# Hybrid RWKV-7 / short-convolution layer on one core: the stage's cross products come first, operands, blocks and values in half as many transfers

## The chip, the core and the metric

The program runs on one NeuronCore of one Trainium2 chip. TensorE (PE) multiplies matrices, VectorE (DVE), ScalarE (ACT) and GpSimd (POOL) work elementwise, SyncE (SP) issues most of the DMA transfers, which 16 DMA engines carry out. The metric is the device time of one execution in microseconds (us), as the median of several runs. The profile is one further execution, recorded by the hardware profiler; its times count from the first instruction.

## The reference

One denoising step of a one-layer backbone over 128 context tokens and 2048 latent tokens, 1024 channels, in float32. Half of the channels go through a bidirectional RWKV-7 scan (8 heads of 64), the other half through a gated short convolution; both share one input and one output projection.

```python
def step(S, inp):
    r_t, w_t, k_t, v_t, kk_t, a_t = inp
    s_kk = jnp.einsum('bdhij,bdhj->bdhi', S, kk_t)
    S = (S * w_t[..., None, :] - s_kk[..., :, None] * (kk_t * a_t)[..., None, :]
         + v_t[..., :, None] * k_t[..., None, :])
    return S, jnp.einsum('bdhij,bdhj->bdhi', S, r_t)
...
y = ys[:, 0] + jnp.flip(ys[:, 1], axis=1)
...
y = y + (bonus[..., None] * vh).reshape(b, t, A_WIDTH)
...
ya = ya.astype(x.dtype) * jax.nn.silu(g_a)
yb = b_gate * _short_conv(c_gate * u_conv, lp['conv_w'], is_latent) * jax.nn.silu(g_b)
u = jnp.concatenate([ya, yb], axis=-1) @ lp['w_out']
return x + gate * u, s_final
```

The outputs are the normalised context, the normalised latents and the final states of the context scan.

## The kernel before

**Phase 1** projects blocks of 384 tokens through the input weights, forms what the scan needs and writes it to DRAM scratch: `ops0`/`ops1` hold, for each chunk of 64 tokens and direction, the four operands of the chunked scan, `vt` the values, `sg` and `q` the gate and the bonus term, `mixT` the convolution branch. This part is hardly touched by the change.

**Phase 2** is the scan. A *stage* s (17 of them, `NST`) is 128 tokens, two chunks for each of the two directions; one chunk of one direction is a *unit* (s, i, d), four to a stage, in the order of `UNITS`. For a unit:

- `load_unit` (L692) loads `kb` (two operands of all heads, 256 KB) and `x` (two 128 KB loads). `kb` has three buffers, `x` twelve.
- `cross` (L704) multiplies them on PE (tile `psG`, one buffer in PSUM); ACT copies the lower block out (`lab`, L715), four small transfers of 16 KB write its two triangular 32x32 halves to DRAM scratch `at` (L721), DVE masks the rest (`abr`, and back into `x`).
- `turn` (L728) transposes `kb` on PE (`psT`) and ACT copies that out (`kbt`).

After the four units of a stage, `inverse` (L737) loads all its blocks from `at` with 128 partitions (`ab`, L742) and inverts them on POOL by elimination (L747 to L762, one `zt` buffer); POOL itself issues four transfers that write the result to DRAM scratch (L767). `merge` (L817) loads that as `zb` (L821), transposes it on DVE (`ws`, L825) and joins the 32x32 halves to 64x64 blocks with two groups of products on PE (`psU`, `psW`). `step` (L856) then carries the state through one chunk of both directions: products `psw`, `psy`, `pst`, then `psu` with the merged blocks, then the updates of state and output. `load_v` (L847) brings its values, four transfers of 64 KB a chunk.

`main` (L1041) interleaves this: while stage s is stepped, the four units of stage s+2 are crossed and its inversion is started, and at the end of stage s the merge of stage s+1 is done. Between these stand pieces of the output projection (`project`, L1005), six matmuls of 512 columns each: first for the convolution half (`psoc`, 17 tiles, up to stage 8), and from stage 9 on for the scan's half (`psoa`), whose tiles are finished two a stage (`finish`, L953, which loads `sg` and `q`) and then pushed as jobs.

**Order.** On PE the order of phase 2 is the order in which the code is written (`Queue`, L638, ties each PE instruction to the one before). The other engines are ordered by the scheduler when the program is built; on the chip each engine, and SP's queue of transfers, runs strictly in that fixed order. A transfer whose wait is not over holds up all that stand behind it on SP. The built program gives SP's transfers eight completion semaphores in turn, so a transfer also waits for the one eight places before it.

## Time and profile before

| | us |
|---|---|
| median of 3 runs | 1896.28 (1894.37 to 1896.54) |
| the profiled execution | 1894.33 |
| its span, first to last instruction | 1892.4 |
| PE busy | 1636.2 (86%) |
| DVE busy | 1050.6 (56%) |
| ACT busy | 641.0 (34%) |
| POOL busy | 595.5 (31%) |
| DMA queue of SP, share of 16 engines | 63.4% |

The page of the profile also gives the largest groups of transfers: x 136 of 128 KB, kb 68 of 256 KB, the writes of `at` 272 of 16 KB, sv 136 of 64 KB, ab 34 of 256 KB, zb 17 of 512 KB. In a timeline row the columns are start, length, engine, line, operation, output tile <- input tiles, size, count, and in brackets the idle time before it and what ended it; "SPq" is SP's queue issuing a transfer, not the transfer itself. A row of windows gives a stretch of the span, its length, the busy time of each engine (with the count of instructions), the granted PE clock, the busy share of the DMA engines and what they moved. Shares over the whole span mix phase 1, which PE fills, with the scan; the scan is to be read by its stages.

### The profile page before, as it was taken

How to read it: one execution, taken by the hardware profiler on the slowest of the kernel's cores; microseconds unless marked ns; L12 is line 12 of the kernel's file. 1: busy time of each engine (PE TensorE's matmuls, PEld its weight loads, DVE VectorE, ACT ScalarE, POOL GpSimd, SP SyncE). 2: the span in 40 equal slices, each digit the busy share in tenths (PEclk: the TensorE clock that was granted, in tenths of full speed). 3: DMA queues.
4: the chain of work that ended last, by engine and by line, in shares of the span. 5: the costliest groups of instructions: out<-in, count | busy, mean ns of one | idle time of the engine just before them, and what ended most of it. 6: DMA issues, size and time to landing. Idle time of an engine off the chain costs nothing.

```text
span 1892.4 us, 41268 instructions
## 1 busy us (share of the span) xinstructions
PE 1636.2 (86%) x16646; PEld 1427.6 (75%) x16646; DVE 1050.6 (56%) x1883; ACT 641.0 (34%) x1284; POOL 595.5 (31%) x1096
## 2 busy tenths in 40 slices
PE   5999999999999999989898788889577668888777
PEld 2998899998899999888798566667466446666665
DVE  6888877446776354776343535344344335455546
ACT  4555544224443122544110232223123223333323
POOL 0122210002211000222056055564565555555600
PEclk7999999999999999999999888889787778788879
DMA  8789997649889434888864755654555534555433
GB/s 342 226 218 243 225 265 251 210 155 177 189 187 217 147 126 145 192 190 201 256 189 152 209 157 165 179 162 136 177 159 161 158 93 110 163 152 154 133 90 123
DMA packets 395022, 339.93 MB, mean 180 GB/s; under 512 B 289032, under 2 KB 340104, under 8 KB 380752
## 3 DMA queue, kind: packets, MB, share of 16 engines
q1 hardware_dynamic: 392656, 332.84, 63.4%
q0 software_dynamic: 2176, 4.46, 1.3%
q8 instruction: 131, 2.15, 0.5%
q14 instruction: 59, 0.48, 0.1%
HBM read 215.68 MB, written 121.52 MB: 178 GB/s over the span
## 4 chain that ended last, share of the span: by engine, by line
PE 34%; DMA 22%; POOL 19%; DVE 12%; issue 6%; SPq 4%; ACT 2%; POOLq 0%; DVEq 0%; ACTq 0%
POOL zt L762 9%; DMA scr_ops<-sp 6%; POOL ztmp L759 6%; DMA ab<-scr_at 3%; DMA scr_zt<-zt 2%; DMA w<-scr_wsp 2%; PE psoa L648 2%; DMA scr_at<-lab 2%; SPq L721 2%; DMA kb<-scr_ops 2%; PE mmgb L159 1%; PE psoc L648 1%; PE mmgb L161 1%; PE mmgb L160 1%; POOL scr_zt L767 1%
## 5 line engine op out<-in xcount | busy, mean ns | idle before, releaser
L762 POOL TENSOR_TENSOR zt<-zt,ztmp 128x30 f32<-128x30 f32 (+7 forms) x510 | 216.3, 424 | 40.0
L759 POOL TENSOR_TENSOR ztmp<-ab,zt 128x60 f32<-128x60 f32 (+7 forms) x255 | 138.6, 543 | 20.0
L723 DVE TENSOR_TENSOR abr<-psG,mx 128x256 f32<-128x256 f32 x68 | 28.8, 423 | 195.0 <-ACT lab L715 194.8
L315 POOL TENSOR_TENSOR shk<-rawl 128x384 f32<-128x384 f32 (+1 forms) x24 | 26.5, 1106 | 319.9 <-ACT rawl L311 319.9
L648 PE MATMUL psG<-x,kb 64*64 64x128 f32 x2176 | 80.8, 288 | 40.0 <-DMA kb<-scr_ops 30.1
L648 PEld LDWEIGHTS psG<-x,kb 64*64 64x64 f32 x2176 | 63.6, 140 | 54.6 <-issue 48.0
L751 POOL COPY dgp<-ab 128x16 f32<-128x16 f32 x17 | 4.5, 264 | 315.6 <-DMA ab<-scr_at 315.5
L648 PE MATMUL psoa<-woh,mh 128*128 128x512 f32 x136 | 66.1, 486 | 37.7 <-ACT mh L1001 37.7
L726 DVE TENSOR_TENSOR x<-psG,mx 64x512 f32<-64x512 f32 x136 | 93.6, 689 | 1.8
L825 DVE STREAM_TRANSPOSE ws<-zb 32x512 f32<-32x512 f32 x34 | 23.8, 701 | 109.5 <-DMA zb<-scr_zt 101.5
L648 PE MATMUL psU<-ws,lab 32*32 32x32 f32 x1088 | 29.9, 219 | 60.3 <-DVE ws L825 56.2
L648 PEld LDWEIGHTS psU<-ws,lab 32*32 32x32 f32 x1088 | 27.0, 134 | 67.9 <-issue 54.3
L1021 DVE TENSOR_TENSOR o<-psoa,gl 128x512 f32<-128x512 f32 x32 | 21.9, 684 | 88.3 <-PE psoa L648 88.3
L159 PE MATMUL mmk<-h,w 128*128 128x384 f32 (+1 forms) x184 | 62.2, 338 | 8.4 <-DMA w<-scr_wsp 8.4
L159 PE MATMUL mmg<-h,w 128*128 128x384 f32 (+1 forms) x192 | 63.6, 331 | 5.8 <-ACT rawc L318 3.4
L159 PE MATMUL mmv<-h,w 128*128 128x384 f32 (+1 forms) x192 | 66.1, 344 | 1.7 <-ACT q1r L313 1.6
L648 PEld LDWEIGHTS psoa<-woh,mh 128*128 128x128 f32 x136 | 29.1, 214 | 50.8 <-ACT mh L1001 39.9
L159 PE MATMUL mmgb<-h,w 128*128 128x384 f32 (+1 forms) x192 | 64.3, 335 | 1.4 <-DMA w<-scr_wsp 1.4
L735 ACT COPY kbt<-psT 128x512 f32<-128x512 f32 x68 | 39.9, 587 | 73.8 <-PE psT L648 73.5
L159 PE MATMUL mmc<-h,w 128*128 128x384 f32 (+1 forms) x192 | 63.9, 333 | 1.1 <-DMA w<-scr_wsp 1.1
L648 PE MATMUL psoc<-woh,mh 128*128 128x512 f32 x136 | 64.0, 471 | 0.7 <-ACT woh L993 0.7
L648 PE MATMUL psoa<-woh,ml 128*128 128x512 f32 x136 | 61.3, 451 | 3.7 <-DVE ml L1002 3.6
(298 smaller groups left out, 5256.8 us busy)
## 6 DMA issues: line engine op xcount, KB each, us to landing
w<-scr_wsp SPq DMA_DIRECT2D x68, 1024.0 KB, 7.7
scr_wsp<-w SPq DMA_DIRECT2D x34, 1024.0 KB, 6.3
wr<-in_win SPq DMA_DIRECT2D x34, 512.0 KB, 6.9
kb<-scr_ops SPq DMA_DIRECT2D x68, 256.0 KB, 3.9
x<-scr_ops SPq DMA_DIRECT2D x136, 128.0 KB, 4.3
scr_ops<-sp SPq DMA_DIRECT2D x80, 192.0 KB, 4.5
scr_ops<-sp SPq DMA_DIRECT2D x160, 96.0 KB, 5.0
ab<-scr_at SPq DMA_DIRECT2D x34, 256.0 KB, 4.1
```

Source lines behind the costliest of these rows:

```text
L159: T.matmul(ps[:, :n], w[:, 0, k], hh[:, 0, k, :n], start=k == 0, stop=False)
L160: T.matmul(ps[:, :n], w[:, 0, k], hh[:, 1, k, :n], start=False, stop=False)
L315: G.tensor_tensor(s[:, lo:n].rearrange("p (r c) -> p r c", c=64), rp[:, :R, 0:64], rp[:, :R, 2:66], ALU.add)
L648: r = f(*args, **kw)
L721: D(at[u0:u0 + 4, h, b].rearrange("u j i -> j u i"), un.lab[r0:r0 + 32, :, b * 32:b * 32 + 32])
L723: V.tensor_tensor(un.abr[:], pb[:, :, 1, :], B.mx[:, 0, 1].unsqueeze(1).broadcast_to((128, 4, 64)), ALU.mult)
L726: V.tensor_tensor(un.x[q, h].rearrange("r a p t -> r p a t"), px[q], B.mx[q, d].unsqueeze(1).broadcast_to((64, 4, 2, 64)), ALU.mult)
L735: P.copy(un.kbt[:], pt[:])
L759: G.tensor_tensor(tv, ab[:, j:j + 2, j + 2:32].unsqueeze(1).broadcast_to((128, kn, 2, n)), zt[:, :kn, j:j + 2].unsqueeze(3).broadcast_to(( ...
L762: G.tensor_tensor(zt[:, :kn, j + 2:32], zt[:, :kn, j + 2:32], tv[:, :, r], ALU.add)
L825: V.transpose(zr[r0], zb[r0, :, 0:32])
L1021: V.tensor_tensor(o[:], ps[:], g[:, cs], ALU.mult)
```

## The change

Four things, all in phase 2 (plus the layout of `vt`, `at` in scratch).

1. **Fewer, larger transfers.** `load_units` replaces `load_unit` and brings both chunks of a direction at once: `kb` 512 KB in one transfer (two buffers of twice the size), `x` in two of 256 KB (six buffers of twice the size). The blocks `lab` of two units share a tile, and their halves are written to `at` after the second one, 32 KB each. `load_v` brings both directions in one transfer for each half of the heads. Per stage: x 8 to 4, kb 4 to 2, writes of `at` 16 to 8, sv 8 to 4.
2. **Cross products first.** In a stage the crosses and turns of stage s+2 no longer stand between the pieces of projection but right behind the first products of each step.
3. **One slot later.** The third part of a merge (`psW`) moves from the end of stage s into stage s+1, behind the first products of its step; three pieces of projection stand behind the merge instead of one; tiles that are finished wait in a list (`waiting`) and become a job when one of two places is free.
4. **Small ones.** The projection's scratch `o` has one buffer instead of two; the four writes of the inverse (L771) read neighbouring partitions instead of every second one.

```diff
@@ -626,7 +626,7 @@
 for _d in range(2):
     SCR[f"ops{_d}"] = (36, 128, 16, 64)
     SCR[f"pc{_d}"] = (512, 34)
-SCR.update(vt=(17, 2, 128, 4, 64), sg=(512, NT), q=(512, NT), mixT=(512, NT))
+SCR.update(vt=(2, 34, 64, 4, 64), sg=(512, NT), q=(512, NT), mixT=(512, NT))
 
 
...
-    def long(un, shape, tag):
-
-        i = un.n % 12
-        return tl(O.r if i < 8 else O.l, shape, f"{tag}{i}", 1)
-
-    def load_unit(s, i, d):
-        un = Ctx()
-        units[s, i, d] = un
-        un.n = (s * 2 + i) * 2 + d
-        src = S[f"ops{d}"][34 + i if s == 0 and d == 1 else 2 * s + i]
-        un.kb = tl(O.r, [128, 4, 2, 64], "kb", 3)
-        un.x = long(un, [128, 2, 2, 4, 64], "x")
-        D(un.kb[:].rearrange("r p k t -> r (p k) t"), src[:, 8:16])
+    def long(n, of, shape, tag):
+
+        i = n % of
+        return tl(O.r if 3 * i < 2 * of else O.l, shape, f"{tag}{i}", 1)
+
+    def load_units(s, d):
+
+        n = 2 * s + d
+        e = 34 if s == 0 and d == 1 else 2 * s
+        src = S[f"ops{d}"][e:e + 2].rearrange("i r k t -> r i (k t)")
+        kb = tl(O.r, [128, 2, 4, 2, 64], "kb", 2)
+        x = long(n, 6, [128, 2, 2, 2, 4, 64], "x")
+        D(kb[:].rearrange("r i p k t -> r i (p k t)"), src[:, :, 512:1024])
         for h in range(2):
-            D(un.x[HR[h], h].rearrange("r a p t -> r (a p) t"), src[HR[h], 0:8])
-        return un
+            D(x[HR[h], :, h].rearrange("r i a p t -> r i (a p t)"), src[HR[h], :, 0:512])
+        for i in range(2):
+            un = Ctx()
+            units[s, i, d] = un
+            un.n = (s * 2 + i) * 2 + d
+            un.kb, un.x = kb[:, i], x[:, i]
...
-        un.lab = tl(O.r, [128, 4, 64], "lab", 8)
-        P.copy(un.lab[:], pb[:, :, 0, :])
-        at = S["at"][s]
-        u0 = i * 8 + d * 4
+        if i == 0:
+            un.labs = tl(O.r, [128, 2, 4, 64], "lab", 4)
+        else:
+            un.labs = units[s, 0, d].labs
+        un.lab = un.labs[:, i]
+        P.copy(un.lab, pb[:, :, 0, :])
         for h in range(2):
-            for b in range(2):
+            for b in range(2 * i):
                 r0 = h * 64 + b * 32
-                D(at[u0:u0 + 4, h, b].rearrange("u j i -> j u i"), un.lab[r0:r0 + 32, :, b * 32:b * 32 + 32])
-        un.abr = long(un, [128, 4, 64], "abr")
+                x = un.labs[r0:r0 + 32, :, :, b * 32:b * 32 + 32].rearrange("j i p c -> j (i p) c")
+                D(S["at"][s, b, d * 8:d * 8 + 8, h].rearrange("u j i -> j u i"), x)
+        un.abr = long(un.n, 12, [128, 4, 64], "abr")
...
-            D(ab[h * 64:h * 64 + 64].rearrange("p j i -> p (j i)"), at.rearrange("u s b j i -> (u s b) (j i)"))
+            D(ab[h * 64:h * 64 + 64].rearrange("p j i -> p (j i)"), at.rearrange("b u h j i -> (b u h) (j i)"))
...
-                G.dma_start(x, zt[c * 64 + b:c * 64 + 64:2])
+                G.dma_start(x, zt[c * 64 + b * 32:c * 64 + b * 32 + 32])
 
     def first(s):
+        for d in range(2):
+            load_units(s, d)
         for k in UNITS:
-            load_unit(s, *k)
             cross(s, *k)
             yield
             turn(s, *k)
...
-        for d in range(2):
-            c = i if d == 0 else 1 - i
-            for h in range(2):
-                x = S["vt"][tile_of(s, d), h, c * 64:c * 64 + 64]
-                D(sv[HR[1 - h], h, d], x)
+        c = [2 * tile_of(s, 0) + i, 2 * tile_of(s, 1) + 1 - i]
+        e = sorted(c)
+        for h in range(2):
+            x = S["vt"][h, e[0]:e[1] + 1:e[1] - e[0]].rearrange("d t p v -> t d p v")
+            q = sv[HR[1 - h], h]
+            D(q if c == e else q[:, ::-1], x)
...
-            o = tl(O.w, [128, 512], "o", 2)
+            o = tl(O.w, [128, 512], "o", 1)
...
+        def refill():
+            while len(jobs) < 2:
+                if convs:
+                    t = convs.pop(0)
+                    x = tl(O.w, [128, 4, 128], "mr", 1)
+                    D(x[:], S["mixT"][:, t * 128:t * 128 + 128].rearrange("(k p) t -> p k t", p=128))
+                    src, att = A["x"], 0
+                elif B.att and waiting:
+                    t, x = waiting.pop(0)
+                    src, att = S["z0"], 1
+                else:
+                    return
+                z = tl(O.w, [128, 1024], "z", 2)
+                D(z[:], src[t * 128:t * 128 + 128, :])
+                jobs.append(project(t, att, parts(x), z))
+
...
+        def finish_a(k):
+            if k < len(fin):
+                next(fin[k][2])
+
+        def finish_b():
+            if fin:
+                t, y, f = fin.pop(0)
+                next(f)
+                waiting.append((t, y))
+                if B.att:
+                    refill()
 
...
             a = step(s, 0)
             next(a), next(a)
-            Rp(2)
-            L(s + 2, 1)
+            next(m, None)
+            C(0)
+            R(0)
             next(a)
-            piece()
-            Rp(3)
-            L(s + 2, 2)
-            C(0)
-            piece()
-            R(0)
-            L(s + 2, 3)
             C(1)
+            R(1)
             next(a), next(a)
-            piece()
-            finish_piece(True)
+            finish_a(0)
             C(2)
             piece()
-            finish_piece(False)
+            R(2)
+            L(0)
             a = step(s, 1)
             next(a), next(a)
-            piece()
-            next(a)
-            R(1)
+            finish_a(1)
             C(3)
             if u:
                 inverse(u)
+            R(3)
+            L(1)
+            next(a)
             piece()
-            finish_piece(True)
+            finish_b()
+            piece()
             next(a), next(a)
-            finish_piece(False)
             piece()
-            L(s + 3, 0)
-            m = merge(s + 1) if s + 1 < NST else iter(())
-            next(m, None)
-            next(m, None)
+            finish_b()
             piece()
-            next(m, None)
+            if s + 1 < NST:
+                m = merges[s + 1] = merge(s + 1)
+                next(m), next(m)
+            piece(3)
```

**SP's queue in a middle stage**: what stands between the load of one stage's inverse (`zb`) and the load of the next stage's blocks (`ab`). Before:

```order
L821 DMA zb_12592<-scr_zt 128x16x64
L721 DMA scr_at<-lab_12461 32x4x32 x4
L854 DMA sv_12677<-scr_vt 64x256
L943 DMA scr_ysp<-y_12310 128x512
L943 DMA scr_ysp<-y_12312 128x512
L742 DMA ab_12471<-scr_at 64x1024 x2
```

and after the change:

```order
L829 DMA zb_13012<-scr_zt 128x16x64
L728 DMA scr_at<-lab_12617 32x8x32 x4
L699 DMA kb_12766<-scr_ops_57 128x2x512
L701 DMA x_1429_12767<-scr_ops_57 64x2x512 x2
L701 DMA x_1439_12909<-scr_ops_59 64x2x512 x2
L728 DMA scr_at<-lab_12666 32x8x32 x4
L699 DMA kb_12908<-scr_ops_59 128x2x512
L749 DMA ab_12839<-scr_at 64x1024 x2
```

All eight writes of `at` and most of the operand loads of the stage after now stand between the two; before, only the last unit's four writes did.

**SP's queue in a late stage** (around the `zb` of stage 12; `sg` and `mr` are the loads of `finish`). Before:

```order
L721 DMA scr_at<-lab_16758 32x4x32 x4
L699 DMA kb_16790<-scr_ops_59 128x512
L821 DMA zb_17191<-scr_zt 128x16x64
L721 DMA scr_at<-lab_16812 32x4x32 x3
L1036 DMA out_y<-z_16489 128x1024
L721 DMA scr_at<-lab_16812 32x4x32
L854 DMA sv_16926<-scr_vt 64x256 x4
L1074 DMA z_17115<-scr_z_68 128x1024
L721 DMA scr_at<-lab_16894 32x4x32 x4
L959 DMA sg_16912<-scr_sg 128x4x128
L959 DMA mr_16913<-scr_q 128x4x128
```

and after the change:

```order
L829 DMA zb_16924<-scr_zt 128x16x64
L863 DMA sv_16635<-scr_vt 64x2x256 x2
L728 DMA scr_at<-lab_16478 32x8x32 x4
L699 DMA kb_16630<-scr_ops_57 128x2x512
L701 DMA x_1707_16631<-scr_ops_57 64x2x512 x2
L701 DMA x_1721_16787<-scr_ops_59 64x2x512 x2
L728 DMA scr_at<-lab_16527 32x8x32 x4
L699 DMA kb_16786<-scr_ops_59 128x2x512
L749 DMA ab_16717<-scr_at 64x1024 x2
L968 DMA sg_16677<-scr_sg 128x4x128
L968 DMA mr_16678<-scr_q 128x4x128
```

The loads of one of the two finishing tiles have moved behind `ab`, and `zb` has the whole queue of the next inversion behind it.

**PE, first half of a middle stage** (`psoc` are pieces of projection, `psT` a turn, `psG` a cross). Before:

```order
L648 MATMUL pst_12718<-sv_12358,idt_8879 64x512 x2
L648 MATMUL psT_12721<-idt_8879,kb_12196 128x128 x4
L648 MATMUL psu_12733<-ws_12700,zb_12592 64x64 x16
L648 MATMUL psoc_12761<-woh_1234_10214,mh_12406 128x512
L648 MATMUL psoc_12761<-wol_1235_10215,mh_12406 128x512
L648 MATMUL psoc_12761<-woh_1234_10214,ml_12407 128x512
L648 MATMUL psoc_12761<-woh_1237_10220,mh_12406 128x512
L648 MATMUL psoc_12761<-wol_1238_10221,mh_12406 128x512
L648 MATMUL psoc_12761<-woh_1237_10220,ml_12407 128x512
L648 MATMUL psT_12768<-idt_8879,kb_12244 128x128 x4
L648 MATMUL psG_12780<-x_1439_12588,kb_12587 64x128 x16
```

and after the change:

```order
L648 MATMUL pst_13672<-sv_13326,idt_8879 64x512 x2
L648 MATMUL psW_13675<-zb_13567,ws_13569 32x32 x32
L648 MATMUL psG_13710<-x_1469_13322,kb_13321 64x128 x16
L648 MATMUL psT_13733<-idt_8879,kb_13321 128x128 x4
L648 MATMUL psu_13740<-ws_13654,zb_13567 64x64 x16
L648 MATMUL psG_13759<-x_1479_13464,kb_13463 64x128 x16
L648 MATMUL psT_13782<-idt_8879,kb_13463 128x128 x4
```

The first two crosses with their turns stand around `psu`; the pieces of projection that stood there have moved towards the end of the stage.

More of the change, by code (lines that the diff above doesn't have):

```diff
@@ L1045, in main @@
         jobs = []
+        waiting = []
         convs = list(range(17))
-        def next_conv():
-            if not convs:
-                return
-            t = convs.pop(0)
-            t0 = t * 128
-            mx = tl(O.w, [128, 4, 128], "mr", 1)
-            D(mx[:], S["mixT"][:, t0:t0 + 128].rearrange("(k p) t -> p k t", p=128))
-            z = tl(O.w, [128, 1024], "z", 2)
-            D(z[:], A["x"][t0:t0 + 128, :])
-            jobs.append(project(t, 0, parts(mx), z))
-        def piece():
-            while jobs:
+        def refill():
[13 more added lines that the diff above has]
+                jobs.append(project(t, att, parts(x), z))
@@ L1077, in main @@
-        B.conv = True
+                    refill()
+        B.att = False
         run = lambda gen: [None for _ in gen]
         run(merge(0))
-        next_conv()
-        next_conv()
-        load_unit(2, *UNITS[0])
+        refill()
+        for d in range(2):
+            load_units(2, d)
         fin = []
-        ctx = None
-        def finish_piece(last):
-            if fin and fin[0][3] == last:
-                f = fin[0]
-                next(f[2])
-                f[3] = True
-                if last:
-                    fin.pop(0)
-                    if f[0] == 0:
-                        B.ctx = f[1]
-                    else:
-                        push(f[0], f[1])
+        merges = {}
@@ L1099, in main @@
+        def finish_a(k):
[7 more added lines that the diff above has]
+                if B.att:
+                    refill()
         for s in range(NST):
             u = s + 2 if s + 2 < NST else None
-            C = lambda k: cross(u, *UNITS[k]) if u else piece()
-            R = lambda k: turn(u, *UNITS[k]) if u else None
-            L = lambda st, k: load_unit(st, *UNITS[k]) if st < NST else None
@@ L1104, in main, with C, R, L @@
-            Rp = lambda k: turn(s + 1, *UNITS[k]) if 0 < s < NST - 1 else None
+            def C(k):
+                if u:
+                    cross(u, *UNITS[k])
+                else:
+                    piece()
+            def R(k):
+                if u:
+                    turn(u, *UNITS[k])
+            def L(d):
+                if s + 3 < NST:
+                    load_units(s + 3, d)
             if s == 9:
-                B.conv = False
                 while jobs or convs:
-                    if not jobs:
-                        next_conv()
```

35 lines of the change are left out of this document (17 added, 18 removed).

## The prediction

> **What bounds the kernel now.** I read the timeline of POOL first, because POOL marks a stage: row L767 writes out the inverse that the next merge needs. These rows mark the inverses of stages 2, 9 and 16.
>
> ```profile
> 1121.68 1.33 POOL L767 DMA_DIRECT2D scr_zt<-zt  x2 [0.29 <-POOL zt L762]
> ...
> 1443.33 0.69 POOL L767 DMA_DIRECT2D scr_zt<-zt  x1 [0.29 <-POOL zt L762]
> ...
> 1794.39 2.61 POOL L767 DMA_DIRECT2D scr_zt<-zt  x4 [0.29 <-POOL zt L762]
> ```
>
> They cut phase 2 into a transition, a middle (seven inversions), a late part (seven) and a tail. The windows give each part its length and busy times: PE, PEld, DVE, ACT, POOL, then clock, DMA share and GB/s.
>
> ```profile
> 1027.50:1121.70 94.20, 66.88 (x1141) 53.30 (x1141) 43.01 (x77) 26.84 (x48) 25.34 (x55) 0.83 0.64 180
> 1121.70:1443.30 321.60, 261.98 (x4590) 204.12 (x4590) 131.54 (x202) 85.54 (x169) 190.19 (x392) 0.87 0.56 159
> 1443.30:1794.40 351.10, 258.67 (x4420) 207.17 (x4418) 166.11 (x298) 105.80 (x218) 194.64 (x393) 0.82 0.53 143
> 1794.40:1892.40 98.00, 72.66 (x794) 57.23 (x788) 51.78 (x108) 30.20 (x70) 2.59 (x4) 0.86 0.34 105
> ```
>
> No engine fills a stage: in the middle PE works 262 of 322 us, POOL 190. So a loop of waits sets the period. Stage 4 to 5 shows it, first on POOL, then in SP's queue.
>
> ```profile
> 1231.88 0.21 POOL L751 COPY dgp<-ab 128x16 f32<-128x16 f32 x1 [10.20 <-DMA ab<-scr_at]
> ...
> 1259.69 2.60 POOL L767 DMA_DIRECT2D scr_zt<-zt  x4 [0.29 <-POOL zt L762]
> 1273.66 0.21 POOL L751 COPY dgp<-ab 128x16 f32<-128x16 f32 x1 [6.15 <-DMA ab<-scr_at]
> ```
>
> ```profile
> 1220.82 0.37 SPq L821 DMA_DIRECT2D zb<-scr_zt  x1
> 1221.29 3.41 SPq L721 DMA_DIRECT2D scr_at<-lab  x4
> ...
> 1226.56 1.09 SPq L742 DMA_DIRECT2D ab<-scr_at  x2
> ...
> 1260.22 1.88 SPq L721 DMA_DIRECT2D scr_at<-lab  x4
> 1266.65 0.38 SPq L821 DMA_DIRECT2D zb<-scr_zt  x1
> 1267.27 2.06 SPq L742 DMA_DIRECT2D ab<-scr_at  x2
> ```
>
> SP issues `zb` only when the inverse of stage s has landed, and the `ab` of stage s+1 stands behind it. POOL inverts (1231.88 to 1259.69, 27.8), the result lands and `zb` goes (7.0 later), `ab` follows after 0.6 to 5.7, and POOL starts 5.3 to 6.4 after that. Seven rounds in 321.6 are 45.9 each. PE runs in the same round: it waits for the merge behind `zb`.
>
> ```profile
> 1226.46 0.28 PE L648 MATMUL psU<-ws,lab 32*32 32x32 f32 x2 [7.04 <-DVE ws L825]
> 1272.34 0.28 PE L648 MATMUL psU<-ws,lab 32*32 32x32 f32 x2 [7.31 <-DVE ws L825]
> ```
>
> In the late part (50.2 a round) PE joins in: `psU` comes later after `zb`, and finishing tiles make it wait, as the list of waits of that part has it (sum, count, longest).
>
> ```profile
> PE psoa L648 <- ACT mh L1001: 30.2, 10, 6.2
> ```
>
> **The change, part by part.**
>
> *Middle, seven rounds.* What now stands between `zb` and `ab` is eight writes of `at`, a `kb` of 512 KB, four `x` of 256 KB and another `kb`. If issuing them sets the time: the first issue after `zb` takes 3.41 for its four (row above), the other four writes 1.88, the gap to `ab` is 1.9 (1224.70 to 1226.56), and operand loads have these rows (of two stretches):
>
> ```profile
> 1236.31 1.82 SPq L701 DMA_DIRECT2D x<-scr_ops  x3
> ...
> 1701.85 0.37 SPq L821 DMA_DIRECT2D zb<-scr_zt  x1
> 1702.31 1.42 SPq L1074 DMA_DIRECT2D z<-scr_z  x1
> 1703.82 3.35 SPq L701 DMA_DIRECT2D x<-scr_ops  x4
> 1707.26 0.54 SPq L699 DMA_DIRECT2D kb<-scr_ops  x1
> 1707.85 3.21 SPq L721 DMA_DIRECT2D scr_at<-lab  x4
> 1713.70 1.09 SPq L742 DMA_DIRECT2D ab<-scr_at  x2
> ```
>
> So 0.45 (`zb`) + 3.41 + 0.5 (`kb`) + 2.5 (four `x` of 0.6) + 1.9 + 1.9 = 10.7: the low end. The high end comes from the same fence, with the sizes of the table of transfers (count, KB each, median us to landing):
>
> ```profile
> kb<-scr_ops SPq DMA_DIRECT2D x68, 256.0 KB, 3.9
> x<-scr_ops SPq DMA_DIRECT2D x136, 128.0 KB, 4.3
> ...
> zb<-scr_zt SPq DMA_DIRECT2D x17, 512.0 KB, 4.6
> ...
> z<-scr_z SPq DMA_DIRECT2D x17, 512.0 KB, 4.5
> ```
>
> `zb`, `z`, four `x`, `kb` and four writes of 16 KB are 1856 KB, and `ab` waited 11.85 (1701.85 to 1713.70) behind them. The new queue has 512 (`zb`) + 256 (writes) + 512 (`kb`) + 1024 (`x`) = 2304 KB up to its last write, so by bytes 14.7. The stretch that carries most in this case,
>
> ```profile
> 1226.00:1227.50 1.50, 0.68 (x17) 0.57 (x19) 1.01 (x2) 0.00 (x0) 0.00 (x0) 0.50 0.93 321
> ```
>
> moves 321 GB/s, and 2304 KB at that are 7.3: bytes needn't set it. I take 13.0, between the ends and nearer the high one, since an `ab` waits for the last write behind all those loads. From `ab` to POOL 5.5 (5.3 and 6.4 above), the inverse 27.8, and from its first write to `zb` 4.4, by stage 14's pair (row below and 1701.85), since nothing late stands ahead of `zb` any more; the middle's own 7.0 had unfinished writes ahead of it.
>
> ```profile
> 1668.54 0.21 POOL L751 COPY dgp<-ab 128x16 f32<-128x16 f32 x1 [16.55 <-DMA ab<-scr_at]
> 1697.44 1.96 POOL L767 DMA_DIRECT2D scr_zt<-zt  x3 [0.31 <-POOL zt L762]
> ```
>
> A round: 13.0 + 5.5 + 27.8 + 4.4 = 50.7. In the order of SP the rounds of stages 3 and 5 have half the writes ahead of `zb`, 1.9 less. 5 x 50.7 + 2 x 48.8 = 351.1 against 321.6: **+29.5** (ends: 10.7 and 5.3 give +12, 14.7 and 6.4 give +48).
>
> *Late, seven rounds.* The inverse takes up to 28.9 here (1668.54 to 1697.44), on average 28.4 by POOL's busy time (194.64 against 190.19 over seven); with 4.4 that is 32.8. From `zb` to POOL the order gives four kinds: stages 10 and 12 have four `x` and four writes behind `zb` (9.5 between an issue sum of 8 and the bytes, + 5.5 = 15.0), stage 11 only four writes (0.4 + 3.5 + 1.9 + 5.5 = 11.3), 13 to 15 the whole queue and two `sv` (14.4 + 5.5 = 19.9), 16 no operands (8.5 + 5.5 = 14.0). Sum 2 x 15.0 + 11.3 + 3 x 19.9 + 14.0 = 115.0, and 7 x 32.8 = 229.6: 344.6 against 351.1, **-6.5**. It rests on PE keeping up. In these rounds the second tile's `sg` and `mr` are issued behind `ab`, so the pieces that stand after `psU` can start only some 15.5 (issue) + 4 (landing, as loads of their size have in the table above) + 3 (an estimate for DVE and ACT's `mh`) = 22.5 after `zb`. A round has 37 us of PE work (258.67 / 7), 36 of it behind `psU`: the next `psU` comes 58.5 after this `zb`. The loop gives 19.9 + 32.8 + 5.7 (1220.82 to 1226.46, `zb` to `psU`) = 58.4. That is a tie, with no slack.
>
> *Transition.* Its `ab` is held up by these loads:
>
> ```profile
> 1073.16 2.54 SPq L870 DMA_DIRECT2D sv<-in_st  x3
> ...
> 1084.96 1.81 SPq L721 DMA_DIRECT2D scr_at<-lab  x4
> 1089.57 1.09 SPq L742 DMA_DIRECT2D ab<-scr_at  x2
> ```
>
> The change crosses stage 2 without projection pieces between, with four `x` issued where there were twelve and four `sv` where there were eight. Eight `x` at 0.6 and four `sv` at 0.6 are 7.2, and some 3 us of pieces stood before the last cross: `ab` at about 1079, **-10.5** (ends 0 and -13.5).
>
> *Tail.* `psU` of the last stage comes 20.5 after its inverse (1794.4, row below), because PE is behind.
>
> ```profile
> 1814.93 1.92 PE L648 MATMUL psU<-ws,lab 32*32 32x32 f32 x64
> ```
>
> By the loop it would come 4.4 + 5.7 = 10.1 after, but the pieces that PE has put off must follow: I take **-6** (ends 0 and -10.4).
>
> *At nothing:* the 18 issues a stage that are saved (11 us of SP) lie where SP waits at `zb` anyway. One buffer of `o` is covered by the other half's three matmuls; without that cover it is under 1 us a piece. `psW` a slot later waits for nothing, since `psU` stands before it by three pieces.
>
> Sum: 1892.4 - 10.5 + 29.5 - 6.5 - 6 = 1898.9 of span, and the profiled execution has 1.9 outside it: 1900.8 against 1894.33, +6.5. On the median 1896.28 that is **1903 us**.
>
> **Rivals.**
>
> *Faster: the number of transfers sets `zb` to `ab`, not bytes.* Then the middle takes the low ends (10.7 and 5.3: +12 in place of +29.5), stages 10 and 12 lose 1.6 each and 13 to 15 2.5 each, 11 together; 17.5 + 11 less than the forecast: **1875**. For it: the stretch with 321 GB/s above. Against it: the 11.85 us with only ten issues in between, of which the issuing itself fills 8.5. [...]
>
> *Slower: PE falls behind in the late rounds.* The tie above breaks: if finished tiles come 4 us later (DVE has the merge and the step before them), the next `psU` is late, the fourth cross with it, and once that cross is later than `zb`, `ab` waits for PE. From there each us costs one; five rounds of 4 give **1923**. For it: `PE psoa` waits for `ACT mh` already. Against it: PE has 13 us idle a late round to take it up.
>
> *Nothing happens.* The middle's loss is about +23, so that gains and losses cancel: **1896**. This lies inside the forecast's own range.
>
> **How the numbers follow.** A measurement of this kernel can tell 0.2% (3.8 us) from no change. Forecast 0.5, with its own range 1890 to 1917: 0.07 of it faster than 1892.5, 0.12 the same (the third rival), 0.31 slower. Fewer transfers 0.29, all faster. PE behind 0.21, all slower. Together 0.36 faster, 0.12 the same, 0.52 slower. The low ends of all terms give 1903 - 28.5 - 3 - 4.4 = 1867, the high ends 1903 + 18.5 + 10.5 + 6 = 1938; I leave about a tenth out on each side: 1868 to 1932.
>
> **What would show it.** After the change the middle's writes L767 should lie 50 to 51 us apart (48 if the first rival is right, over 52 by bytes), `ab` 12 to 14 behind `zb`, `POOL dgp` waiting for `ab` with about 20 us a stage. PE should wait longer for `ws` in the middle. In the late part rounds of about 49 with `psU` 6 behind `zb` show the loop in charge; `psU` over 12 behind it, with `psoa` waiting for `mh`, shows the second rival. The first `ab` of the transition should go near 1079. I am wrong if the middle's rounds are at or under 46: then the loads don't delay `ab`, or the order on SP isn't what paces it.

## The result and the profile after

| | before | after |
|---|---|---|
| median, us (5 runs each, taken together) | 1896.54 | 1912.77 |
| ratio, 95% interval | | 1.0072 (1.0047 to 1.0098) |
| profiled span, us | 1892.4 | 1911.0 |
| PE busy, us | 1636.2 | 1622.5 |
| DVE / ACT / POOL busy, us | 1050.6 / 641.0 / 595.5 | 1053.6 / 641.4 / 583.3 |

The changed kernel is slower by 0.7%, although PE and POOL are busy for less. The writes of the inverses of stages 2, 9 and 16 now begin at 1118.8, 1466.7 and 1814.8; cut there, the windows of the changed kernel answer to those shown of before (PE, PEld, DVE, ACT, POOL, clock, DMA share, GB/s):

```profile
1027.50:1118.80 91.30, 69.07 (x1240) 57.27 (x1240) 40.94 (x74) 28.38 (x51) 24.65 (x54) 0.85 0.62 168
1118.80:1466.70 347.90, 268.33 (x4655) 213.62 (x4654) 129.42 (x205) 87.87 (x174) 180.86 (x393) 0.85 0.58 153
1466.70:1814.80 348.10, 250.05 (x4352) 197.58 (x4352) 174.97 (x306) 105.46 (x217) 195.48 (x393) 0.85 0.54 141
1814.80:1911.00 96.20, 65.99 (x726) 50.78 (x724) 50.76 (x101) 27.83 (x63) 2.59 (x4) 0.86 0.35 110
```

| part | before | forecast | after | forecast change | change |
|---|---|---|---|---|---|
| transition | 94.2 | 83.7 | 91.3 | -10.5 | -2.9 |
| middle | 321.6 | 351.1 | 347.9 | +29.5 | +26.3 |
| late | 351.1 | 344.6 | 348.1 | -6.5 | -3.0 |
| tail | 98.0 | 92.0 | 96.2 | -6.0 | -1.8 |
| sum | | | | +6.5 | +18.6 |

The whole loss lies in the middle, whose rounds went from 45.9 to 49.7 us. By the rows of all fourteen rounds, the stretch from `zb` to `ab` grew by 7.2 us on average (6.6 to 13.8), while the rest of the loop shrank by 3.4: the inverse by 1.3, from its first write to `zb` by 1.8, from `ab` to POOL by 0.3. One round of the changed kernel, the longest of the seven, first on POOL, then in SP's queue:

```profile
1168.66 2.60 POOL L774 DMA_DIRECT2D scr_zt<-zt  x4 [0.30 <-POOL zt L769]
...
1193.01 0.21 POOL L758 COPY dgp<-ab 128x16 f32<-128x16 f32 x1 [19.08 <-DMA ab<-scr_at]
...
1219.40 2.60 POOL L774 DMA_DIRECT2D scr_zt<-zt  x4 [0.30 <-POOL zt L769]
```

```profile
1173.00 0.38 SPq L829 DMA_DIRECT2D zb<-scr_zt  x1
1173.43 3.21 SPq L728 DMA_DIRECT2D scr_at<-lab  x4
1176.74 0.40 SPq L699 DMA_DIRECT2D kb<-scr_ops  x1
1177.24 2.54 SPq L701 DMA_DIRECT2D x<-scr_ops  x4
1179.88 2.48 SPq L728 DMA_DIRECT2D scr_at<-lab  x4
1182.98 0.38 SPq L699 DMA_DIRECT2D kb<-scr_ops  x1
1188.19 1.11 SPq L749 DMA_DIRECT2D ab<-scr_at  x2
```

From `zb` to `ab` it is 15.2 here, POOL stands for 19.1 us, and the round is 50.7. The issues themselves are done after 9.4 us (1182.36). The remaining 5.8 pass until the last writes of `at`, queued behind 1.5 MB of operands, have landed. The list of waits of the middle of the changed kernel (sum, count, longest) shows the same wait on two engines, and a third that is new:

```profile
POOL dgp L758 <- DMA ab<-scr_at: 126.0, 7, 19.1
...
DVE ws L833 <- DMA zb<-scr_zt: 86.7, 7, 13.9
...
PE psoc L648 <- DVE o L1030: 59.2, 7, 10.0
```

The third invites a wrong reading: `o` has one buffer now, and PE waits for `o`. But PE does not write `o`: it waits for its PSUM tile `psoc`, which the operation on `o` has to read first. The rows of DVE and of PE at that place (changed kernel, stage 4) tell it otherwise:

```profile
1228.65 1.42 DVE L833 STREAM_TRANSPOSE ws<-zb 32x512 f32<-32x512 f32 x2 [13.63 <-DMA zb<-scr_zt]
1230.10 0.69 DVE L1030 TENSOR_TENSOR o<-psoc,gl 128x512 f32<-128x512 f32 x1
```

```profile
1230.84 0.80 PE L648 MATMUL psoc<-woh,mh 128*128 128x512 f32 x1 [9.75 <-DVE o L1030]
...
1233.70 1.92 PE L648 MATMUL psU<-ws,lab 32*32 32x32 f32 x64
```

DVE stands at the transpose of `zb`; the `o` behind it in DVE's order is ready (the last product before PE's wait ends at 1221.09) and starts at 1230.10, when the transposes are done. It is the old wait for the merge, met one piece of projection earlier. In loads_behind (below), where `o` has one buffer too, this wait is 5.6 us in the middle instead of 59.2.

### The profile page after: what moved, and what is told of

The parts are those of the page before. It is cut to its first block, busy times and chain, and to the rows that moved or that the text cites. A ratio compares the mean times of both kernels' runs of the same rounds, so it can differ in the third digit from the quotient of the medians.

```text
span 1911.0 us, 40886 instructions
## 1 busy us (share of the span) xinstructions
PE 1622.5 (85%) x16646; PEld 1418.5 (74%) x16646; DVE 1053.6 (55%) x1883; ACT 641.4 (34%) x1284; POOL 583.3 (31%) x1096
## 4 chain that ended last, share of the span: by engine, by line
PE 37%; DMA 21%; POOL 16%; DVE 13%; issue 6%; SPq 4%; ACT 2%; DVEq 0%; POOLq 0%; ACTq 0%
POOL zt L769 8%; DMA scr_ops<-sp 6%; POOL ztmp L766 5%; DMA kb<-scr_ops 3%; DMA ab<-scr_at 3%; DMA scr_at<-lab 3%; PE psoa L648 2%; DMA w<-scr_wsp 2%; PE mmgb L159 2%; PE mmc L159 2%; PE mmgb L161 2%; PE mmgb L160 2%; PE mmb L161 2%; PE mmc L161 2%; PE mmc L160 2%
## 5 line engine op out<-in xcount | busy, mean ns | idle before, releaser
L769 POOL TENSOR_TENSOR zt<-zt,ztmp 128x30 f32<-128x30 f32 (+7 forms) x510 | 204.4, 401 | 40.0
L766 POOL TENSOR_TENSOR ztmp<-ab,zt 128x60 f32<-128x60 f32 (+7 forms) x255 | 140.7, 552 | 20.0
L648 PE MATMUL psoc<-woh,mh 128*128 128x512 f32 x136 | 65.2, 480 | 59.2 <-DVE o L1030 59.2
L648 PE MATMUL psG<-x,kb 64*64 64x128 f32 x2176 | 87.2, 292 | 11.6 <-issue 4.6
L648 PEld LDWEIGHTS psG<-x,kb 64*64 64x64 f32 x2176 | 68.7, 143 | 22.0 <-issue 16.4
L648 PEld LDWEIGHTS psoc<-woh,mh 128*128 128x128 f32 x136 | 29.3, 215 | 70.5 <-DVE o L1030 62.2
L648 PE MATMUL psT<-idt,kb 128*128 128x128 f32 x272 | 48.3, 305 | 28.4 <-ACT zb L848 26.1
L159 PE MATMUL mmgb<-h,w 128*128 128x384 f32 (+1 forms) x192 | 64.0, 333 | 3.2 <-DMA w<-scr_wsp 3.2
L161 PE MATMUL mmgb<-h,w 128*128 128x384 f32 (+1 forms) x192 | 63.8, 332 | 0.1
L160 PE MATMUL mmgb<-h,w 128*128 128x384 f32 (+1 forms) x192 | 63.7, 332 | 0.0
L648 PEld LDWEIGHTS psT<-idt,kb 128*128 128x128 f32 x272 | 32.6, 151 | 41.7 <-ACT zb L848 29.6
```

The source lines that it names most:

```text
L159: T.matmul(ps[:, :n], w[:, 0, k], hh[:, 0, k, :n], start=k == 0, stop=False)
L160: T.matmul(ps[:, :n], w[:, 0, k], hh[:, 1, k, :n], start=False, stop=False)
L161: T.matmul(ps[:, :n], w[:, 1, k], hh[:, 0, k, :n], start=False, stop=k == 7)
L648: r = f(*args, **kw)
L766: G.tensor_tensor(tv, ab[:, j:j + 2, j + 2:32].unsqueeze(1).broadcast_to((128, kn, 2, n)), zt[:, :kn, j:j + 2].unsqueeze(3).broadcast_to(( ...
L769: G.tensor_tensor(zt[:, :kn, j + 2:32], zt[:, :kn, j + 2:32], tv[:, :, r], ALU.add)
```

## The experiments

Each ratio is against the kernel before, in runs on the same chip. The three groups ran on three chips (before was 1892.1, 1893.9 and 1892.1 there), so kernels of different groups are compared by ratio.

### First group: is it SP's queue, and what in it?

**zb_pool** lets POOL issue `zb`:

```diff
-        D(zb[:], S["zt"][s % 3].rearrange("u h r c -> (h r) u c"))
+        G.dma_start(zb[:], S["zt"][s % 3].rearrange("u h r c -> (h r) u c"))
```

> The changed kernel, but zb is issued by POOL, which has just written the inverse, instead of by SP. Theory A (SP's queue standing still at zb is the loss of the middle): the writes of at and ab of the next stage go as soon as the blocks are there, ab has landed before POOL wants it, and a middle round falls from 49.7 us to POOL's own 31 (inverse 26.5, its landing and the start of the next 4 to 5) or to what PE needs, 40 to 43; the late part falls from 348 to 300-325. In all 1911 to between 1810 and 1850 us. Theory B (PE sets the middle's rounds by the pieces of projection and crosses that now stand elsewhere; SP's queue is only where it shows): middle rounds stay at 48 to 50, in all 1900 to 1915.

Measured: 1870.68, ratio 0.9900 (0.9868 to 0.9932). Faster than both kernels, but the middle's rounds only fell to 45.9 (321.0 in seven). Theory B is out, and theory A is incomplete. A round of zb_pool in SP's queue and on POOL:

```profile
1195.60 2.15 SPq L728 DMA_DIRECT2D scr_at<-lab  x4
1197.80 0.46 SPq L699 DMA_DIRECT2D kb<-scr_ops  x1
1198.35 2.75 SPq L701 DMA_DIRECT2D x<-scr_ops  x4
1201.20 3.48 SPq L728 DMA_DIRECT2D scr_at<-lab  x4
1205.76 0.38 SPq L699 DMA_DIRECT2D kb<-scr_ops  x1
1211.18 1.11 SPq L749 DMA_DIRECT2D ab<-scr_at  x2
```

```profile
1204.86 0.53 POOL L754 MEMSET zt<- 128x512 f32 x1 [6.13 <-DMA scr_zt<-zt]
1205.41 1.17 POOL L829 DMA_DIRECT2D zb<-scr_zt  x1
```

SP no longer stands still, and `ab` still goes 6.5 us after the last `at` has been issued (5.8 in the round of the changed kernel): here too 1.5 MB of operands stand ahead of these writes. And POOL now waits 6.1 for its own writes of `zt` to land, where it was 1.80 in the changed kernel. SP issues `kb` and four `x` while they are under way here (1197.80 to 1201.10), and in the changed kernel it issues nothing from 1159.35 until `zb` goes at 1173.00. So the writes seem to be held up by the operand loads, though another queue issued them: 6.1 against 1.8 us.

**loads_behind** keeps `zb` on SP and ties `kb` and `x` behind `ab` in SP's order:

```diff
+        if s > 2:
+            for q in r:    # r: the loads of kb and x
+                tc.add_manual_dep(q.ins, B.ab.name, NoSync)
...
-            L(0)
             a = step(s, 1)
...
                 inverse(u)
             R(3)
+            L(0)
             L(1)
```

> The changed kernel, with the loads of kb and x put behind ab in SP's order, so that only eight writes of at stand between zb and ab. Theory A with issue times: zb 0.4 + 3.4 + 2 + 1.9 = 7.8 from zb to ab in place of 13 to 14, five and a half less in seven middle rounds and in three late ones: about 1860 us (1850 to 1875). Theory A with the eight writes alone being slow to land: zb to ab 11 to 12, about 1890. Theory B (PE): rounds as they are, 1905 to 1915; slower than 1915 if the crosses now wait for kb and x.

Measured: 1844.74, ratio 0.9756 (0.9725 to 0.9787), 3.1% under the changed kernel by the two ratios. The queue of SP in one of its rounds, and the windows of its middle and late part:

```profile
1205.10 0.38 SPq L835 DMA_DIRECT2D zb<-scr_zt  x1
1205.53 5.01 SPq L734 DMA_DIRECT2D scr_at<-lab  x8
1212.62 1.75 SPq L755 DMA_DIRECT2D ab<-scr_at  x2
```

```profile
1111.50:1418.90 307.40, 255.65 (x4702) 205.89 (x4698) 136.53 (x208) 88.46 (x176) 181.54 (x392) 0.90 0.66 171
1418.90:1744.20 325.30, 253.85 (x4424) 199.40 (x4422) 174.59 (x306) 106.63 (x220) 198.52 (x393) 0.88 0.62 154
```

The time lies below the range of theory A (1850 to 1875). `zb` to `ab` is 7.5 here and 7.7 on average (7.8 was worked out), from the end of the last write's issue to `ab` pass 1.5 us on average (2.1 here), and the middle is 40.5 shorter than in the changed kernel. That is more than the change had cost there (26.3). The late part gives 22.8, more than expected, the transition 7.3: there the first `ab` goes at 1078.9, where the prediction had put it for the change (1079).

**small_ops** loads and writes per unit again, in the changed order:

```diff
+        for i in range(2):
+            D(kb[:, i].rearrange("r p k t -> r (p k t)"), src[:, i, 512:1024])
+            for h in range(2):
+                D(x[HR[h], i, h].rearrange("r a p t -> r (a p t)"), src[HR[h], i, 0:512])
...
-            for b in range(2 * i):
+            for b in range(2):
+                D(S["at"][s, b, u0:u0 + 4, h].rearrange("u j i -> j u i"), un.lab[r0:r0 + 32, :, b * 32:b * 32 + 32])
```

> The changed kernel, with kb and x loaded per unit again (kb 256 KB, x 128 KB) and the blocks written per unit (16 KB): twice the transfers, the same bytes, order of PE as changed. In SP's order seven x, four kb and eight writes stand between zb and ab where four x, two kb and eight writes did. If the bytes ahead of ab set the time: zb to ab 13 to 14 as it is, in all within 10 of 1911. If each issue costs: 2.5 to 3 us more a round, in all 1925 to 1935. If the larger transfers themselves were the loss: zb to ab 9 to 10 as before, 1885 or less.

Measured: 1929.98, ratio 1.0203 (1.0160 to 1.0246). The total is what a price per issue would give, the place is not. Its middle and late part:

```profile
1119.20:1463.40 344.20, 267.05 (x4622) 212.25 (x4622) 128.28 (x203) 87.19 (x173) 180.90 (x392) 0.85 0.56 153
1463.40:1833.80 370.40, 255.92 (x4397) 202.49 (x4396) 175.99 (x307) 107.61 (x222) 194.00 (x393) 0.82 0.50 135
```

In the middle four more issues stand between `zb` and the last write of `at`, with 256 KB less, and the time is 3.7 less: a price of each issue is not seen there. One of its rounds in SP's queue:

```profile
1172.96 0.39 SPq L830 DMA_DIRECT2D zb<-scr_zt  x1
...
1182.14 2.30 SPq L729 DMA_DIRECT2D scr_at<-lab  x4
...
1185.62 1.09 SPq L750 DMA_DIRECT2D ab<-scr_at  x2
```

The last four writes begin later after `zb` than in the changed kernel (9.2 us for 6.9 in the round shown there), and `ab` goes sooner (12.7 for 15.2). In the late part it takes 22 more. All of it lies between `zb` and POOL's start (139.2 us over the seven rounds where it was 116.0): in stages 13 to 15 that is 21.7 to 24.0 where it was 20.1 to 21.0, and the most is lost in stages 10 and 11 (19.2 and 17.7 for 15.2 and 11.4), where the built order puts loads or writes ahead of `ab` that don't stand there in the changed kernel. So the late part does not show a price per issue by itself either.

**before_zb_pool** makes the edit of zb_pool in the kernel before.

> The kernel before, with zb issued by POOL. Theory A: here too the queue of SP no longer stands still; middle rounds fall from 45.9 us to 40 to 42 (PE, 37.4 busy), the late ones, where PE is late too, from 50.2 to 45 to 48: 1896 to between 1830 and 1860. Theory B: 1885 to 1900.

Measured: 1881.8, ratio 0.9948 (0.9925 to 0.9971): a miss. Its middle rounds are 45.2 (45.9 before). `zb` to POOL takes 9.6 instead of 12.1 on average, but `zb` itself goes 7.6 after the inverse's first write instead of 6.1. SP's queue is not what the rounds of the kernel before hang on alone.

### Second group: how short can the loop be?

**blocks_first** is loads_behind, and ties `zb` behind the writes of `at`:

```diff
+        r = D(zb[:], S["zt"][s % 3].rearrange("u h r c -> (h r) u c"))
+        tc.add_manual_dep(r.ins, B.at.name, NoSync)    # B.at: the last write of at
```

> The changed kernel with kb and x behind ab, and zb behind all eight writes of at too: nothing stands between zb and ab. Theory A alone: a round of the loop is 0.6 + 5 + 26.5 + 4.4 = 36.5, less than PE's 37 to 40, so PE sets a middle round of 40 to 42 (43.9 with the eight writes between); the late part, where PE is late already, gains at most 10. 1815 to 1835 us. If PE sets the 43.9 already: 1840 to 1848.

Measured: 1816.27, ratio 0.9595 (0.9552 to 0.9639), inside the range worked out. Its queue of SP in one round, and its middle and late part:

```profile
1200.97 0.38 SPq L835 DMA_DIRECT2D zb<-scr_zt  x1
1201.65 1.93 SPq L755 DMA_DIRECT2D ab<-scr_at  x2
```

```profile
1111.20:1398.30 287.10, 254.32 (x4696) 204.91 (x4695) 136.02 (x210) 87.80 (x175) 187.57 (x392) 0.94 0.71 185
1398.30:1720.20 321.90, 249.58 (x4425) 195.53 (x4423) 178.56 (x305) 106.68 (x220) 201.70 (x392) 0.89 0.61 154
```

A middle round is 41.0, and PE is busy for 36.3 of it. But PE does not set it, as the expectation had it. In the last six of the seven rounds the loop alone gives 40.3: `zb` goes 4.8 after the inverse's first write (4.3 is the least in any run), `ab` 0.7 behind it, POOL starts 7.5 behind that (5 were expected; in the changed kernel, where `zb` goes 13.8 ahead of the blocks instead of 0.7, it is 5.1, and that the 512 KB of `zb` hold them up was not tried by itself), and the inverse takes 27.4 (26.5). The expected 36.5 was too short, and the total came out right by luck. The late part hardly moved (321.9 for 325.3): in its last rounds `zb` waits for writes whose cross comes late, so it no longer hangs on SP's queue.

**behind_small** is loads_behind with the small transfers of small_ops.

> The changed kernel with the operand loads behind ab, but kb and x per unit again and the blocks written per unit: twice the transfers, in a place where SP has time. If size and number are worth nothing there: 1838 to 1852, as with the large ones. If each of the 20 further issues a stage costs something even there: 1860 or more. If the small ones land sooner and that matters: under 1835.

Measured: 1852.43, ratio 0.9781 (0.9746 to 0.9817), against 0.9756 for loads_behind. The intervals overlap: out of the loop's way, the size of the transfers is worth 0.25% by the two ratios, which can't be told from nothing.

**behind_pool** is loads_behind with `zb` issued by POOL.

> The changed kernel with the operand loads behind ab and zb issued by POOL, so SP stands still for no inverse. Theory A: as blocks_first, since ab is even earlier: 1815 to 1835. If POOL's wait for its own writes to land (some 4 us more a round) or another wait of SP (the value loads, as in zb_pool) takes the place: 1840 to 1860.

Measured: 1833.01, ratio 0.9679 (0.9637 to 0.9721): at the slow end of what theory A gave, with rounds of 43.0 in the middle. With the operands behind `ab`, POOL gets `zb` out 5.6 to 7.4 after the inverse, not 8 to 10 as in zb_pool. Keeping `zb` on SP behind the blocks is better.

**before_first** ties `zb` behind the writes of `at` in the kernel before.

> The kernel before, with zb behind all its writes of at and nothing else changed. Theory A: the middle's round loses most of the 6.4 that lie between zb and ab on average, so 40 to 42, 27 to 35 less; in the late part, where PE comes late, 0 to 20 less: 1850 to 1870. If it is as fast as blocks_first (within 8), crosses first, later merges and larger transfers earn nothing by themselves; if it is 20 or more slower, they earn that. If it is 1885 or more, theory A fails for the kernel before.

Measured: 1872.08, ratio 0.9896 (0.9860 to 0.9932): 2 us above theory A's range, and the middle did not do what theory A said. Its middle:

```profile
1115.90:1435.70 319.80, 273.97 (x4653) 213.64 (x4653) 131.08 (x210) 88.80 (x174) 189.74 (x392) 0.87 0.58 167
```

The middle is nearly as it was (321.6). Of the 17.9 us between the profiled spans, 10.2 lie in the late part (340.9 for 351.1) and 5.8 ahead of the middle. In the order before, the fourth cross comes too late for a `zb` that waits for the blocks: the inverse of stage 4 is written out at 1209.9, the last `lab` of stage 5 comes at 1216.9, and `zb` goes at 1221.1. The rest of the change, with its operand loads behind `ab`, therefore earns 56 us once nothing stands between `zb` and `ab` (1872.08 against 1816.27, same chip).

### Third group: what earns it, and can it be better?

**first_merge_early** puts `psW` back at the stage's end, in blocks_first:

```diff
-            next(m, None)
             C(0)
...
                 next(m), next(m)
-            piece(3)
+            piece()
+            next(m, None)
+            piece(2)
```

> blocks_first, with psW back at the end of the stage (one piece of projection behind psU, two behind it), as the kernel before had it. If the later slot is worth what it saves PE (ACT's copy of the merged half, about 1 to 2 us a stage): 1820 to 1840. If it is worth nothing: within 8 of blocks_first (1816). If psW so late delays the step: under 1808.

Measured: 1795.28, ratio 0.9492 (0.9459 to 0.9525), the fastest of all, 5.1% under before: the third case of the expectation. The later slot costs some 20 us (1.0% by the two ratios, 21.5 us between the profiled spans). Its middle and late part, and then one row each from the waits of the middle of blocks_first and of the late parts of blocks_first and first_merge_early:

```profile
1107.70:1392.50 284.80, 255.23 (x4683) 204.29 (x4681) 136.43 (x206) 86.54 (x172) 186.46 (x392) 0.93 0.71 186
1392.50:1703.00 310.50, 255.02 (x4469) 202.59 (x4466) 174.99 (x309) 109.10 (x224) 198.99 (x393) 0.88 0.62 162
```

```profile
PE psT L648 <- ACT zb L855: 14.1, 7, 4.7
```

```profile
PE psoa L648 <- ACT mh L1017: 35.8, 10, 11.0
```

```profile
PE psoa L648 <- ACT mh L1017: 19.1, 5, 4.0
```

With `psW` in the step, the next turn waits for ACT's copy of `psW` (they share the one PSUM buffer of tag "t"), 2 us a stage, and this wait is gone from the middle of first_merge_early. Only 2.3 us of the gain lie in that middle, though, whose rounds the loop sets. Of the 21.5 us, 11.4 lie in the late part, where PE waits 17 us less for the finished tiles, 4.3 in the tail, 3.5 ahead of the middle. That the shorter wait for `mh` follows from the merge's place is argued from these rows, not tried by itself.

**first_crosses_late** puts three pieces of projection ahead of the first three crosses, in blocks_first:

```diff
+            piece()
             C(0)
             R(0)
             next(a)
+            piece()
             C(1)
...
+            piece()
             C(2)
...
-            piece(3)
```

> blocks_first, with the three pieces of projection that stand behind the merge put ahead of the first three crosses instead (the crosses are late again, the transfers large, the queue of SP as in blocks_first). If the early crosses are what makes the blocks ready before the inverse: the fourth lab comes some 9 us later, zb waits for it, middle rounds go from 40.7 to 44-46 and the whole to 1845-1875 (before_first: 1872). If larger transfers are what earns it: within 10 of 1816.

Measured: 1820.75, ratio 0.9618 (0.9600 to 0.9637), not told apart from blocks_first. But the run does not test what it was meant to. The fourth `lab` did not come late: in the middle it ends 0.7 us behind the inverse's first write on average, 0.8 in blocks_first, and 6.8 in before_first. Moved from behind one merge to ahead of the next crosses, the pieces still stand between that merge and the fourth cross. So whether the early crosses earn the 56 us stays open; that the blocks are ready 6 us sooner than in before_first speaks for it. The size of the transfers earns little of it, if anything (behind_small). The loads asked for a whole stage ahead, the turns right behind their crosses and the finishing tiles' order were not taken apart either.

**first_tiles_first** puts `kb` and `x` of the late stages behind the `sg` and `mr` of the finishing tile, in blocks_first:

```diff
+                if s > 12:
+                    tc.add_manual_dep(q.ins, B.sg.name, NoSync)    # B.sg: the last of sg, mr
```

> blocks_first, with kb and x of the late stages behind the sg and mr of the finishing tile instead of ahead of them (2 MB less in front of these loads). If PE's late rounds are set by that tile's loads: PE waits 3 to 5 us less for mh in five stages, 1795 to 1808. If by the chain of the tile through DVE and ACT: within 6 of 1816. If kb and x now come late for the first cross: over 1822.

Measured: 1818.72, ratio 0.9608 (0.9592 to 0.9625), the same as blocks_first: these loads are not what the late rounds wait for. The `sg` of a late stage goes no sooner for it (8.7 us behind `ab` in the round of stage 15, 8.5 in blocks_first), and PE's wait for `mh` in the late part is 35.8 us in both.

**before_o1** gives the kernel before one buffer of `o`.

> The kernel before, with one buffer of the projection's scratch o instead of two, nothing else. The prediction put it at nothing: within 6 us of before. If PE's pieces wait for the release of o (1 us in each of 68): 1905 to 1940.

Measured: 1893.30, ratio 1.0020 (0.9995 to 1.0044): nothing that can be told apart, as the prediction had priced it. No run gives the changed kernel its second `o` back.

## Why the prediction was right, and where it was not

**What bounds it: right.** The loop inverse, `zb`, `ab`, inverse paced the middle, and the order of SP set its length. blocks_first, loads_behind and the changed kernel are three lengths of the queue between `zb` and `ab` (0.7, 7.7 and 13.8 us on average) with middle rounds of 41.0, 43.9 and 49.7. Between the last two, 6.1 us of queue give 5.8 us of round. Between the first two, 6.9 us give only 2.9, and the rest is lost again in the same loop: POOL starts 2.3 later after `ab`, the inverse takes 0.9 longer, `zb` goes 0.8 later. The 0.6 to 5.7 from `zb` to `ab` that I read off two rounds of before were not all of them: over its seven middle rounds it is 0.6 to 15.9.

**The middle, +29.5 forecast, +26.3 measured: the right mechanism, and a size from two errors that cancel, so in part luck.** `zb` to POOL came to 132.4 over the seven rounds where I had 7 x 18.5 - 2 x 1.9 = 125.7: `zb` to `ab` took 14.2 in the five full rounds (I had 13.0) and 12.8 in the rounds of stages 3 and 5 (11.1), and `ab` to POOL 0.4 a round less than I had. The inverse took 26.4 a round where I had carried over 27.8 from before, 9.6 less in all. The choice of 13.0, between issuing alone (10.7) and bytes alone (14.7), was the step on which everything hung, and it was a choice, not worked out. What was measured lies near the bytes. Up to the last write of `at` 2267 KB stand in this queue on average, `zb` included, and `ab` goes after 13.8 us; in small_ops it is 2039 KB and 12.4 us, although the last write is issued 10.4 us after `zb` there and 8.7 here. Both are 6.2 us per MB (1024 KB). That the bytes set it is read from these averages; no run changed the bytes alone. Loads_behind, with 768 KB, takes 7.7, where issuing counts. The 321 GB/s by which I took bytes not to matter were not at hand: from `zb` to `ab` in the round shown the DMA engines moved 190 GB/s, at a busy share of 0.81.

**Late, -6.5 forecast, -3.0 measured: right, round by round.** Forecast 47.8, 44.1, 47.8, 52.7, 52.7, 52.7, 46.8; measured 47.9, 44.3, 48.1, 53.5, 53.3, 53.7, 47.4. The tie with PE was called too favourably. `psU` came 19 to 24 us behind `zb` from stage 11 on, not 5.7. The 3 us put down for DVE and ACT's `mh` held: behind the `zb` of stage 13 in the changed kernel DVE takes up the `sg` issued behind `ab` at 1687.02, and `mh` is done at 1690.06. But that is 25.2 behind `zb` (1664.83), where I had 22.5. The list of waits of the late part of the changed kernel has

```profile
PE psoa L648 <- ACT mh L1010: 62.5, 9, 20.1
```

which is the sign that the prediction gave to its slower rival. But that rival's price did not come. A constant lag is no longer period: the crosses were still in time, and loads_behind shortened the rounds of stages 13 to 15 from 53.3 to 53.7 down to 46.2 to 50.8, with `psU` as late as before. So in these the loop was still in charge, with some 3 to 7 us to spare before PE. (The last round went from 47.4 to 49.9 there, since its fourth `lab` came 11 us after the inverse's first write.)

**Tail, -6 forecast, -1.8 measured: mis-sized by that same lag.** The last `psU` came 24.7 after its inverse, later than the 20.5 before, where I had taken some 14.5. What was gained lies behind it: from this `psU` to the end 71.5 us instead of 77.5, which I did not have. In the tail PE has 6.7 us less to do (65.99 for 72.66).

**Transition, -10.5 forecast, -2.9 measured: the step that failed.** I counted what the change takes out of the stretch (eight `x`, four `sv`, pieces of projection) and not what it puts between the last writes. The rows of the changed kernel:

```profile
1073.74 3.18 SPq L728 DMA_DIRECT2D scr_at<-lab  x4
1077.01 0.40 SPq L699 DMA_DIRECT2D kb<-scr_ops  x1
1077.51 2.55 SPq L701 DMA_DIRECT2D x<-scr_ops  x4
1080.15 2.20 SPq L728 DMA_DIRECT2D scr_at<-lab  x4
1083.19 0.38 SPq L699 DMA_DIRECT2D kb<-scr_ops  x1
1087.43 1.11 SPq L749 DMA_DIRECT2D ab<-scr_at  x2
```

It is the queue that I had priced for the middle: `ab` at 1087.4, not 1079. loads_behind moved it to 1078.9.

**The faster rival (fewer transfers count, not bytes) was wrong** for the middle: small_ops has four more issues there, 256 KB less, and is 3.7 us faster in it. **The rest at nothing** held for `o` in the kernel before (before_o1), but not for `psW`: its products wait for nothing, but others wait for it, and in blocks_first its place costs some 20 us. In the middle of the changed kernel PE waits 19.2 us there as well (`psT` for ACT's copy of `psW`, seven times). What that costs the changed kernel, where the loop sets the rounds, wasn't tried.

In short: 0.7% slower, where 0.3% was forecast, for the reason given; the missing 12 us are the gains of transition, late part and tail, sized 15.3 us too large, less the 3.2 by which the middle lost less than I had.

## What to carry to other kernels

When a change moves work "earlier" or merges transfers, look in the built order at what now stands in each queue between the two ends of the tightest loop: 1.5 MB of loads that nobody needed yet cost more than the rest of the change earned, and tying them behind the loop's own transfer turned 0.7% slower into 2.4% faster than before. Price such a queue by the bytes ahead of its last small write (here some 6.2 us per MB), and by issuing plus one landing where that is longer (5.4 + 2.1 us in the round of loads_behind, whose 768 KB would be 4.7). And when PE is shown waiting for a buffer, look at what the releasing engine itself stood at before giving that buffer a second copy.

## What the hardware showed that I had not expected

- Small writes landed later with big loads ahead of them: between the end of the last issue of `at` and `ab` lay 5.8 us with operands ahead and 2.1 without (1188.19 - 1182.36 in the changed kernel, 1212.62 - 1210.54 in loads_behind; 4.8 and 1.5 on average of the seven middle rounds). Issuing `zb` from another queue did not get round it (6.5 in the round of zb_pool).
- After PE's wait of 9.75 us the 512-column matmuls of the changed kernel start 0.43 us apart until 1239.5, for 8.7 us (with `psU`, 64 products of 32 columns, in 1.9 of them), and then 0.22 to 0.26 apart as before the wait. The granted clock is 0.50 in that stretch and 1.00 behind it:

```profile
1237.85 0.63 PE L648 MATMUL psoc<-woh,ml 128*128 128x512 f32 x1
1238.28 0.63 PE L648 MATMUL psoc<-woh,mh 128*128 128x512 f32 x1
...
1239.56 0.43 PE L648 MATMUL psoc<-woh,mh 128*128 128x512 f32 x1
1239.82 0.40 PE L648 MATMUL psoc<-wol,mh 128*128 128x512 f32 x1
```

  In the wait itself it is 1.00 up to 1225.9 and 0.50 from 1226.0 on. Before the full clock is back, PE works without a gap: 2.9 us of 512-column matmuls, 1.9 of `psU`, 4.0 of 512-column matmuls again. So this wait cost PE more than its length: 15 matmuls that start 0.43 apart instead of some 0.23 are some 3 us more, an estimate from these rows. The kernel with the shorter waits also ran at the higher granted clock: in the middle PE is idle for 79.6 us at 0.85 in the changed kernel and for 32.8 at 0.94 in blocks_first, and over the whole it is 0.918 and 0.936; that the waits make the difference was not tried by itself.
- The inverse on POOL is not of fixed length: seven of them keep POOL busy for 190.2 in the middle before, 180.9 after. Taken place by place in the inverse (45 operations of L766 and L769, means over all 17 inverses of the changed kernel), the records sum to 18.8 us where DVE is idle and to 22.0 where DVE works beside them for over half their length. So in these records the inverse is faster while DVE stands; that DVE is the cause was not tried by itself.
